# A hybrid encoder on one core: weight differences tied to a later tile of the weight stream

## The chip, the core and the metric

The kernel runs on one core of a Trainium2 chip. Its time is the device time of one execution in microseconds (us). The engines named below are TensorE (PE; its weight loads are listed apart as PEld), VectorE (DVE), ScalarE (ACT), GpSimd (POOL) and SyncE (SP). DMAs are issued from SP's and ACT's queues; a line "SPq" or "ACTq" in the profile is such an issue, and it stands in its engine's program order.

## The reference

Two encoder layers run over 272 tokens (16 meta tokens and 256 real ones) of width 2048, in float32. Cut to what matters here:

```python
h = rmsnorm(x); q, k, v, f, ga, gf = split(h @ W_in)
a = attention(q, k, v) @ W_attn_br          # grouped heads, rotary positions
s = real(fft2(f)) @ W_four                  # over positions and group channels
x = x + (sigmoid(ga) * a + sigmoid(gf) * s) @ W_out
up = rmsnorm(x) @ W_up                      # 2048 -> 2 x 5632
x = x + (silu(dwconv3(up[gate])) * up[val]) @ W_down
```

The weights of both layers are read once; the output is the 256 real tokens after the second layer.

## The kernel before

**Weights as a stream.** All weight matrices are cut into tiles of 128 x 1024 numbers (512 KB). One list, `order`, fixes the sequence of all tiles over the whole kernel. A tile `i` goes through three steps: `load_raw` fetches it by a DMA from SP into one of four `raw` buffers; `split_w` has ACT cast it to `wh` (line 230, its high part in the fast float32 format) and DVE subtract to get `wl` (line 233, the low part); then PE multiplies with both. `wh` and `wl` have three buffers each, so a cast waits until PE is done with the tile three places before it. `advance` and `pump` emit the split of a tile two tiles ahead of the one that PE works on.

**Products.** `group` runs one group of tiles: for each 128 x 128 block three matmuls, high x high, high x low and low x high (lines 304 to 306), 24 matmuls in a tile when the moving side is 272 tokens wide. After every second block it calls `step()` and `pump()`, so there are four steps to a tile. `st["cur"]` holds the `wh` of the tile that PE is on.

**Side work.** `step()` moves side work forward: generators yield the number of steps that they want to wait. `weight_sums` is one of these. It is put into the list `behindhand` when the feed-forward stage of the first layer begins, with 24 steps to wait, and so runs beside the `ug`, `uv` and `d` groups of that layer (gate half, value half, down projection).

**The weight differences.** In the second layer a part of the down projection is done as a product of 2 x 2 blocks with seven multiplications instead of eight (a Strassen form, `PRODUCTS`). It needs differences of weight blocks, which are made here ahead of time: for each of 16 rounds `q`, four blocks `b0` to `b3` of 128 x 1024 numbers are loaded from `w_blk`, four differences are made on DVE, and these are stored to device memory (`tsum`), where the second layer reads them as weight tiles. Loads and stores (lines 977 and 982) are issued from ACT's queue. Ahead of each load, a copy of one column from `st["cur"]` into the buffer (line 976) ties the load to a place in the weight stream. A difference (line 980) is emitted nine steps after the load of its second block.

**Who sets the order.** Within the limits of data and buffers, a planner lays down the order of the instructions on each engine when the program is built, by its own costs for each; an instruction may come earlier on its engine than it stands in the code, if by these costs its inputs are there. On the chip each engine then goes through its list in that order.

**Places.** Tiles are put at byte places in the order in which their pools are opened: `per` and `wp` first, then `small`, then a pool for each stage (`mix`, `ffn`). Tables such as `WL_AT`, `X_AT` and `G_AT` set the offsets of operands within their buffers by some tens of bytes.

Of the kernel before, what the change touches and what calls it, by code (L numbers as in the profile page):

```python
# [10 lines left out]
F32 = mybir.dt.float32  # L11
F32R = mybir.dt.float32r
AF = mybir.ActivationFunctionType
ALU = mybir.AluOpType
AX = mybir.AxisListType

P = 128
D = 2048
# [17 lines left out]
NPR = sum(FF_SPLIT[-1][:2]) // 2  # L36
# [84 lines left out]
def encoder_kernel(ctx, tc, xT, params, consts, bmat, w_in, w_abr, w_four, w_f64, w_out, w_up, w_down, w_blk, outT):  # L121
    nc = tc.nc
    dram = ctx.enter_context(tc.tile_pool(name="dram", bufs=1, space=bass.MemoryType.DRAM))
    tsum = [[dram.tile([P, D // 2], F32, name=f"ts{q}_{e}") for e in range(4)] for q in range(NPR)]
# [58 lines left out]
    st = {"raw": 0, "fetch": 0, "next": 0, "grp": 0}  # L183
# [13 lines left out]
    def advance(upto):  # L197
        while st["raw"] < min(upto + RAW, len(chunks)):
            load_raw(st["raw"])
            st["raw"] += 1  # L200
        while st["fetch"] < min(upto, len(chunks)):
            i = st["fetch"]
            if i in folded:
                todo.append((i, lambda i=i: fold_w(i)))
            todo.append((i, lambda i=i: split_w(i, 0, CW)))
            st["fetch"] += 1
# [14 lines left out]
    def split_w(i, a, b, eng=None):  # L221
        if i not in splits:
            h = wp.tile([P, CW, MG * P], F32R, tag="wh", name=f"wh{i}")
            lo = wp.tile([P, CW * MG * P + 64], F32R, tag="wl", name=f"wl{i}")
            o = wl_at[i]
            splits[i] = h, lo[:, o:o + CW * MG * P].rearrange("p (c m) -> p c m", c=CW)
        h, lo = splits[i]
        r = raws[i]
        if eng is None:
            nc.scalar.copy(h[:, a:b], r[:, a:b])  # L230
        else:
            eng.tensor_copy(h[:, a:b], r[:, a:b])
        nc.vector.tensor_tensor(lo[:, a:b], r[:, a:b], h[:, a:b].bitcast(F32), op=ALU.subtract)  # L233
        if b == CW:
            del raws[i]
# [112 lines left out]
    def first_groups(pss):  # L348
# [17 lines left out]
        for i, c0, c1, ks in ((0, 0, 1, (0,)), (0, 1, 2, (1,)), (1, 0, 2, ()), (0, 2, 4, (2, 3)), (1, 2, 4, ())):  # L366
            for k in ks:
                norm_split(k, P_NM)
            split_w(i, c0, c1, nc.vector if (i, c0) == (0, 0) else None)
# [56 lines left out]
    small = ctx.enter_context(tc.tile_pool(name="small", bufs=4))  # L426
# [92 lines left out]
    for l in range(DEPTH):  # L519
# [7 lines left out]
        with tc.tile_pool(name=f"mix{l}", bufs=1) as mp:  # L527
# [394 lines left out]
            for half in range(2):  # L922
                mH = mL = None
                for kind, i in BRANCH_ORDER[half]:
# [19 lines left out]
                    else:  # L944
# [6 lines left out]
                        for m in range(MG):  # L951
                            k = 2 * j + m
                            t_, h_ = tha[i][:, m, lo:T], mH[:, k, lo:T]
# [13 lines left out]
        with tc.tile_pool(name=f"ffn{l}", bufs=1) as fp:  # L967
# [2 lines left out]

            def weight_sums():
                tt = nc.vector.tensor_tensor
                for q in range(NPR):
                    b = [fp.tile([P, D // 2], F32, tag=f"b{e}", name=f"b{e}") for e in range(4)]
                    for e, sums in ((0, ()), (1, ((0, 1, 0, 0),)), (3, ((1, 3, 1, 1), (3, 3, 0, 2))), (2, ((2, 2, 3, 3),))):
                        nc.scalar.copy(b[e][:, 0:1], st["cur"][:, 0, 0:1].bitcast(F32))
                        nc.scalar.dma_start(b[e], w_blk[2 * q + e // 2, e % 2])
                        yield 9
                        for o, x, y, to in sums:
                            tt(b[o], b[x], b[y], op=ALU.subtract)  # L980
                            yield 2
                            nc.scalar.dma_start(tsum[q][to], b[o])
                        yield 3

            sets, prods = [], {"have": {}}
            if last:
# [79 lines left out]
            if l == DEPTH - 2:  # L1066
                behindhand.append([24, weight_sums()])
# [142 lines left out]
```

## Time and profile before

| | |
|---|---|
| runs | 2525.16, 2524.92 and 2531.62 us, median 2525.16 |
| the profiled execution | 2528.11 us, its span 2526.0 us |
| granted PE clock, mean | 0.999 |
| busy: PE, DVE, ACT | 99%, 73%, 51% of the span |
| DMA | 557.63 MB, mean 221 GB/s |
| loads of `b`, stores of `ts` | 64 and 64 of 512 KB, 5.0 and 3.6 us to landing (median) |

The span runs from the first to the last instruction. A row of a group lists line, engine, operation, output and inputs, shapes and count, then busy time and the mean of one in ns, then the idle time of the engine ahead of these instructions and who ended most of it. A row of a wait lists who waited for whom, the total, how often and the longest. A row of a timeline lists start, length, engine, line and operation, and in brackets the idle time before it and what ended it.

### The profile page before, as it was taken

What the parts mean: (1) busy time and instruction counts of PE and PEld (TensorE: products, weight loads), DVE (VectorE), ACT (ScalarE), POOL (GpSimd) and SP (SyncE); (2) the same over time, 40 slices, a digit from 0 to 9 for tenths busy, and PEclk for the clock granted to TensorE, in tenths of its full rate; (3) what the DMA queues carried; (4) which work ended last, traced back from release to release, by engine and by line L of the source; (5) the groups of instructions that cost most, each with busy time, mean ns of one, the idle gap of its engine ahead of it and who ended that gap; (6) DMA issues with size and microseconds to landing.
All of it is one profiled execution on the core that took longest, in us unless ns stands there. A gap on an engine that the chain in (4) does not pass through costs nothing.

```text
span 2526.0 us, 47879 instructions
## 1 busy us (share of the span) xinstructions
PE 2511.2 (99%) x19404; PEld 2441.2 (97%) x19404; DVE 1852.2 (73%) x2851; ACT 1276.4 (51%) x1857; POOL 18.3 (1%) x37
## 2 busy tenths in 40 slices
PE   9999999999999999999999999999999999999999
PEld 9999999999999999999999999999999989988888
DVE  7687867776776556676556887677766788879985
ACT  6455544554444334444444564445644565556653
POOL 0000000000000000000000000000000000000000
PEclk9999999999999999999999999999999999999999
DMA  7545666568888887787554555666656677778875
GB/s 240 166 157 161 194 185 190 189 225 283 286 282 281 277 292 266 270 288 266 183 179 151 175 157 188 196 201 200 188 189 192 217 243 247 244 249 256 260 244 174
DMA packets 157501, 557.63 MB, mean 221 GB/s; under 512 B 18144, under 2 KB 22112, under 8 KB 157280
## 3 DMA queue, kind: packets, MB, share of 16 engines
q1 hardware_dynamic: 134480, 482.54, 59.5%
q10 hardware_dynamic: 22800, 72.04, 8.1%
q8 instruction: 152, 2.49, 0.4%
q14 instruction: 69, 0.57, 0.1%
HBM read 516.07 MB, written 35.65 MB: 218 GB/s over the span
## 4 chain that ended last, share of the span: by engine, by line
PE 95%; DVE 2%; DMA 1%; ACT 1%; issue 1%; ACTq 0%; SPq 0%; DVEq 0%
PE ps_ug L306 6%; PE ps_ug L304 6%; PE ps_uv L300 6%; PE ps_ug L305 6%; PE ps_x L1046 6%; PE ps_d L306 4%; PE ps_d L304 4%; PE ps_d L305 4%; PE ps_uv L301 3%; PE ps_uv L306 3%; PE ps_uv L304 3%; PE ps_uv L305 3%; PE ps_o L304 2%; PE ps_o L306 2%; PE ps_o L305 2%; PE ps_gf L304 2%
## 5 line engine op out<-in xcount | busy, mean ns | idle before, releaser
L233 DVE TENSOR_TENSOR wl<-raw,wh 128x1024 fp32r<-128x1024 f32 (+1 forms) x883 | 1073.8, 1220 | 442.5 <-ACT wh L230 438.2
L230 ACT CAST wh<-raw 128x1024 fp32r<-128x1024 f32 (+1 forms) x882 | 920.9, 1046 | 853.6 <-PE ps_ug L305 171.4
L306 PE MATMUL ps_ug<-xHL,wl 128*128 128x272 f32 (+1 forms) x1408 | 397.6, 282 | 2.7 <-DVE wl L233 2.7
L304 PE MATMUL ps_ug<-xHL,wh 128*128 128x272 f32 (+1 forms) x1408 | 399.1, 283 | 0.0
L305 PE MATMUL ps_ug<-xHL,wh 128*128 128x272 f32 (+1 forms) x1408 | 397.1, 282 | 0.0
L306 PEld LDWEIGHTS ps_ug<-xHL,wl 128*128 128x128 f32 x1408 | 264.5, 188 | 3.1 <-DVE wl L233 3.1
L305 PEld LDWEIGHTS ps_ug<-xHL,wh 128*128 128x128 f32 x1408 | 264.8, 188 | 2.2
L304 PEld LDWEIGHTS ps_ug<-xHL,wh 128*128 128x128 f32 x1408 | 264.3, 188 | 2.7
L300 PE MATMUL ps_uv<-xHL,wh 128*128 128x512 f32 x704 | 247.7, 392 | 0.0
L306 PE MATMUL ps_d<-gHL,wl 128*128 128x272 f32 (+1 forms) x728 | 208.3, 286 | 2.5 <-DVE wl L233 2.5
L304 PE MATMUL ps_d<-gHL,wh 128*128 128x272 f32 (+1 forms) x728 | 208.8, 287 | 0.0
L305 PE MATMUL ps_d<-gHL,wh 128*128 128x272 f32 (+1 forms) x728 | 207.4, 285 | 0.0
L304 PE MATMUL ps_uv<-xHL,wh 128*128 128x272 f32 x704 | 201.3, 286 | 0.0
L306 PE MATMUL ps_uv<-xHL,wl 128*128 128x272 f32 x704 | 200.7, 285 | 0.0
L305 PE MATMUL ps_uv<-xHL,wh 128*128 128x272 f32 x704 | 199.9, 284 | 0.0
L301 PE MATMUL ps_uv<-xHL,wl 128*128 128x256 f32 x704 | 198.3, 282 | 0.0
L300 PEld LDWEIGHTS ps_uv<-xHL,wh 128*128 128x128 f32 x704 | 132.0, 188 | 28.6
L1046 PE MATMUL ps_x<-wh,cb 128*128 128x512 f32 x448 | 156.6, 393 | 0.0
L304 PE MATMUL ps_ga<-xHL,wh 128*128 128x272 f32 (+1 forms) x512 | 147.0, 287 | 0.0
L304 PE MATMUL ps_gf<-xHL,wh 128*128 128x272 f32 (+1 forms) x512 | 145.8, 285 | 0.1
L304 PE MATMUL ps_o<-mH,wh 128*128 128x272 f32 (+1 forms) x512 | 144.6, 282 | 0.0
L306 PE MATMUL ps_ga<-xHL,wl 128*128 128x272 f32 (+1 forms) x512 | 144.6, 282 | 0.0
(306 smaller groups left out, 5979.8 us busy)
## 6 DMA issues: line engine op xcount, KB each, us to landing
raw<-in_w_up SPq DMA_DIRECT2D x352, 512.0 KB, 4.4
raw<-in_w_in SPq DMA_DIRECT2D x206, 512.0 KB, 3.6
raw<-in_w_down SPq DMA_DIRECT2D x112, 512.0 KB, 4.3
raw<-in_w_out SPq DMA_DIRECT2D x64, 512.0 KB, 3.9
b<-in_w_blk ACTq DMA_DIRECT2D x64, 512.0 KB, 5.0
ts<-b ACTq DMA_DIRECT2D x64, 512.0 KB, 3.6
raw<-ts SPq DMA_DIRECT2D x64, 512.0 KB, 4.5
raw<-in_w_blk SPq DMA_DIRECT2D x48, 512.0 KB, 4.4
```

The costliest lines, as they stand in the source:

```text
L230: nc.scalar.copy(h[:, a:b], r[:, a:b])
L233: nc.vector.tensor_tensor(lo[:, a:b], r[:, a:b], h[:, a:b].bitcast(F32), op=ALU.subtract)
L300: nc.tensor.matmul(o2, h[:, c, sl], ab, start=kt == 0, stop=False)
L301: nc.tensor.matmul(o, lo[:, c, sl], ab[:, 0, :], start=False, stop=kt == nk - 1)
L304: nc.tensor.matmul(o, h[:, c, sl], a, start=kt == 0, stop=False)
L305: nc.tensor.matmul(o, h[:, c, sl], b, start=False, stop=False)
L306: nc.tensor.matmul(o, lo[:, c, sl], a, start=False, stop=kt == nk - 1)
L1046: nc.tensor.matmul(ps[e], cb[:, s_, q - q4], w, start=q == 0 and a == 0, stop=q == n - 1 and a == 2)
```

## The change

The first feed-forward stage still makes the same differences from the same blocks. In `split_w`, `st["new"]` now remembers the `wh` of the newest tile whose split has been emitted. In `weight_sums`, the differences of a block are no longer emitted behind its own load. They are kept in a list `due`, and come five steps after the load of the next block. Ahead of them ACT writes a column `one`: the value 1.0, computed as 0 x (first column of `st["new"]`) + 1.0, so that it cannot be written before that tile's cast. The difference is then a `scalar_tensor_tensor` on DVE, `x * one - y`, which reads this column. Two differences that fall due together share one column. The steps between the parts are set so that each of the four blocks of a round takes 12 steps (they were 12, 14, 16 and 14), and one last part round makes the last difference. `one` has two buffers of 128 bytes in the pool `small`, 256 bytes in all, so that the pools behind it move by 256 bytes.

```diff
@@ split_w
             o = wl_at[i]
+            st["new"] = h
             splits[i] = h, lo[:, o:o + CW * MG * P].rearrange("p (c m) -> p c m", c=CW)
@@ weight_sums
-                for q in range(NPR):
-                    b = [fp.tile([P, D // 2], F32, tag=f"b{e}", name=f"b{e}") for e in range(4)]
+                b, due = {}, []
+                for q in range(NPR + 1):
                     for e, sums in ((0, ()), (1, ((0, 1, 0, 0),)), (3, ((1, 3, 1, 1), (3, 3, 0, 2))), (2, ((2, 2, 3, 3),))):
-                        nc.scalar.copy(b[e][:, 0:1], st["cur"][:, 0, 0:1].bitcast(F32))
-                        nc.scalar.dma_start(b[e], w_blk[2 * q + e // 2, e % 2])
-                        yield 9
-                        for o, x, y, to in sums:
-                            tt(b[o], b[x], b[y], op=ALU.subtract)
-                            yield 2
-                            nc.scalar.dma_start(tsum[q][to], b[o])
-                        yield 3
+                        if q < NPR:
+                            t_ = fp.tile([P, D // 2], F32, tag=f"b{e}", name=f"b{e}")
+                            nc.scalar.copy(t_[:, 0:1], st["cur"][:, 0, 0:1].bitcast(F32))
+                            nc.scalar.dma_start(t_, w_blk[2 * q + e // 2, e % 2])
+                        yield 5
+                        if due:
+                            one = small.tile([P, 32], F32, tag="one", name="one", bufs=2)[:, 0:1]
+                            nc.scalar.activation(one, st["new"][:, 0, 0:1].bitcast(F32), AF.Identity, bias=1.0, scale=0.0)
+                        for o, x, y, to in due:
+                            nc.vector.scalar_tensor_tensor(o, x, one, y, op0=ALU.mult, op1=ALU.subtract)
+                            yield 3
+                            nc.scalar.dma_start(to, o)
+                        if q == NPR:
+                            return
+                        b[e] = t_
+                        yield 7 - 3 * min(len(due), 2)
+                        due = [(b[o], b[x], b[y], tsum[q][to]) for o, x, y, to in sums]
```

## The prediction

> **What bounds the kernel now.** I read the page first (busy times and the chain that ended last), then the waits of TensorE (PE) alone, then busy time by stretches of the span, then the order of instructions around one wait. From the page:
>
> ```profile
> span 2526.0 us, 47879 instructions
> ...
> PE 2511.2 (99%) x19404; PEld 2441.2 (97%) x19404; DVE 1852.2 (73%) x2851; ACT 1276.4 (51%) x1857; POOL 18.3 (1%) x37
> ...
> PE 95%; DVE 2%; DMA 1%; ACT 1%; issue 1%; ACTq 0%; SPq 0%; DVEq 0%
> ```
>
> PE is the bound; VectorE (DVE) and ScalarE (ACT) have room. The edit adds no matmul and takes none away, so it can move the time only through moments in which PE stands still or runs slower. Its place is the first layer's feed-forward stage. All waits of PE from 525 to 1300 us are these:
>
> ```profile
> PE ps_ug L306 <- DVE wl L233: 2.7, 2, 1.7
> PE ps_d L306 <- DVE wl L233: 2.5, 1, 2.5
> ```
>
> Three waits, 5.2 us, each for the low part `wl` of a weight tile. Busy time by stretch (columns: length, then busy time and instruction count of each engine, granted PE clock, DMA share, GB/s):
>
> ```profile
> 530.00:700.00 170.00, 170.00 (x1392) 169.92 (x1391) 122.22 (x166) 81.73 (x120) 0.85 (x1) 1.00 0.80 278
> 700.00:1010.00 310.00, 310.00 (x2537) 309.83 (x2536) 201.79 (x240) 134.36 (x181) 0.00 (x0) 1.00 0.82 279
> 1010.00:1197.00 187.00, 181.86 (x1470) 181.22 (x1469) 129.31 (x170) 84.03 (x122) 0.00 (x0) 0.99 0.80 274
> 1197.00:1300.00 103.00, 103.00 (x845) 103.00 (x844) 59.78 (x78) 47.30 (x64) 0.00 (x0) 1.00 0.57 186
> 1187.00:1191.00 4.00, 4.00 (x21) 4.00 (x21) 3.36 (x6) 1.72 (x5) 0.00 (x0) 0.57 0.93 310
> ```
>
> Undisturbed, one matmul takes 310/2537 = 0.1222 us, and 103/845 = 0.1219 us with the differences gone: their traffic by itself does not slow PE. Between 1010 and 1197 us, 1470 matmuls should have taken 1470 x 0.1222 = 179.6 us and took 187: **7.4 us lost**. 5.2 us are the three waits; another 1.4 us lie behind the last of them, where the granted clock is 0.57 and 21 matmuls run in 4 us instead of 32.7; 0.8 us go in starting again.
>
> What is late in the last wait is seen in its order on ACT, DVE and PE:
>
> ```profile
> 1176.38 0.34 ACTq L977 DMA_DIRECT2D b<-in_w_blk  x1
> 1177.91 1.22 DVE L233 TENSOR_TENSOR wl<-raw,wh 128x1024 fp32r<-128x1024 f32 x1
> 1184.35 1.23 DVE L980 TENSOR_TENSOR b<-b,b 128x1024 f32<-128x1024 f32 x1 [4.86 <-DMA b<-in_w_blk]
> 1185.49 1.22 DVE L233 TENSOR_TENSOR wl<-raw,wh 128x1024 fp32r<-128x1024 f32 x1
> 1186.04 1.04 ACT L230 CAST wh<-raw 128x1024 fp32r<-128x1024 f32 x1 [6.63 <-DVE b L980]
> 1186.77 0.39 PE L306 MATMUL ps_d<-gHL,wl 128*128 128x272 f32 x1 [2.46 <-DVE wl L233]
> ```
>
> The difference L980 stands on DVE one `wl` split behind the issue of its load, waits 4.86 us for that load, and holds the next split; its store, issued from ACT, holds the next cast for 6.63 us. Over the stage:
>
> ```profile
> DVE b L980 <- DMA b<-in_w_blk: 69.3, 44, 4.9
> ACT wh L230 <- DVE b L980: 30.2, 8, 6.6
> DMA to landing us min/median/max: 3.4/5.0/7.9
> 1169.50 1.23 DVE L980 TENSOR_TENSOR b<-b,b 128x1024 f32<-128x1024 f32 x1 [3.74 <-DMA b<-in_w_blk]
> ```
>
> (The third row is that of the loads at L977.) 44 of 64 differences wait, but only three reach PE: a hold of 3.74 us still costs nothing, one of 4.86 us costs 2.46 us.
>
> **The change, part by part.** *Distance.* Steps of the generator come every six matmuls, 6 x 0.1222 = 0.733 us, four to a tile, so a tile lasts 2.93 us. Loads are anchored on the tile under multiplication (`cur`); they come at steps 24 + 12k, the last step of a tile t. The sum comes 17 steps later, in the first step of tile t+5, and its column is written from the newest split, t+6. The planner that lays down the order of each engine can therefore put load and difference no closer than six tiles, 6 x 2.93 = 17.6 us; so far it put them about two apart, though 9 steps lie between them in the program. Against a longest landing of 7.9 us the load is in with 9.7 us to spare, even if it is issued two tiles late (3.8 us then). I take the whole of the 69.3 us of waits as gone, with the three that reach PE and the slow clock behind the last: **-7.4 us**. Bounds: 0 (something else holds DVE as long) and -7.4 us.
>
> *Next late.* Then the split itself waits only for its cast, which PE paces. The column is an ACT instruction just behind the cast that DVE also needs for the `wl` of that tile; the column's 0.19 us passes while DVE does that split, so the wait for it should be near zero.
>
> *New and changed instructions.* From the groups of the stage:
>
> ```profile
> L233 DVE TENSOR_TENSOR wl<-raw,wh 128x1024 fp32r<-128x1024 f32 x262 | 320.6, 1224 | 170.1 <-ACT wh L230 169.1
> L230 ACT CAST wh<-raw 128x1024 fp32r<-128x1024 f32 x262 | 274.2, 1047 | 297.1 <-PE ps_d L305 123.2 <-PE ps_ug L305 77.7 <-PE ps_uv L305 41.0
> L980 DVE TENSOR_TENSOR b<-b,b 128x1024 f32<-128x1024 f32 x64 | 78.4, 1224 | 69.7 <-DMA b<-in_w_blk 69.3
> L1130 DVE TENSOR_TENSOR gHL<-cv,gHL 128x272 fp32r<-128x272 f32 x44 | 19.2, 436 | 2.2 <-ACT gHL L1129 1.5
> L480 DVE SCALAR_TENSOR_TENSOR xHL<-XT,prm,xHL 128x272 fp32r<-128x272 f32 x15 | 7.4, 495 | 0.0
> L976 ACT COPY b<-wh 128x1 f32<-128x1 f32 x64 | 12.1, 189 | 1.5
> L1111 ACT ACT_TABLE_LOAD x1 | 1.3, 1283 | 0.0
> ```
>
> 48 columns (three of four blocks in each of 16 rounds) at about 0.19 us, the copy at L976, are 9 us of ACT; Identity runs beside Silu in this stage already, with one table load in all, so I add none. 64 differences become scalar_tensor_tensor. At 272 elements that form takes 495 against 436 ns; if the 59 ns are fixed it is 1.28 us, if they grow with length 1.224 x 495/436 = 1.39 us, and 1.22 us if they vanish. I take 1.28: +4 us of DVE (0 to +11). Both are covered: DVE is busy 122.22 + 201.79 + 129.31 = 453 of 667 us, ACT 300. Without that cover the most they would add is 9 + 11 = 20 us.
>
> *Pace.* A round had 12 + 14 + 16 + 14 = 56 steps and has 4 x 12 = 48, so the stage of differences ends at step 24 + 768 + 8 = 800 instead of 920. Loads and stores are as many as before:
>
> ```profile
> L977 ACTq DMA_DIRECT2D b<-in_w_blk x64: 334/339/344, 533.1 to 1191.2; - x64
> q10 hardware_dynamic: 18288, 66.59, 27.9%
> 1191.00:1195.00 4.00, 4.00 (x35) 4.00 (x34) 2.56 (x3) 2.03 (x4) 0.00 (x0) 1.00 0.97 352
> DMA to landing us min/median/max: 3.3/4.6/7.8
> ```
>
> From the first load, 776 steps or 569 us are left: 66.6 MB plus 194 weight tiles of 0.524 MB (101.7) make 296 GB/s, where 279 ran without a PE wait and 352 were reached for 4 us. The last row is the landing of the weight tiles: they have four buffers, so 4 x 2.93 - 1.05 - 1.22 = 9.4 us from issue to use, against 7.8 us at the worst. I take 0. The last load moves from 1191 to about 533 + 756 x 0.733 = 1087 us.
>
> *Places.* The 256 bytes move every tile of the later pools by the same amount; no row shows what a shift does, so I take 0.
>
> *Sum.* The profiled execution took 2528.11 us (span 2526.0 and 2.1 around it): 2528.11 - 7.4 = 2520.7, with 0.3 for small new waits 2521.0. The three runs shown have a median of 2525.16, 2.95 us under the profiled one, so an ordinary run seems to carry some 4.5 us of these waits. Against the median the forecast is -4.2 us, 0.17%; I call 0.3% (7.6 us) the least that a measurement of this kernel tells from no change.
>
> [...] The row has the granted clock fall to 0.57 behind a PE wait of 2.46 us. [...] The trace speaks for the wait as its cause, since no other stretch of this stage shows a lower clock.
>
> **The rivals.** *Another hold takes the place (about 2527 us).* The next round's copy into `b0` must wait for the second of two differences (`b3 - b0`), which shares its column with the first. Behind the same cast DVE does one split and two differences, 1.22 + 2 x 1.28 = 3.8 us, just what PE bore (3.74). If the planner puts that copy ahead of the next cast, ACT holds it so long in each of 16 rounds; 0.4 us each, half a split, make 6.4 us: 2520.7 + 6.4 = 2527. For it: ACT stood behind DVE 30.2 us in eight places. Against it: there a DMA was in the hold, here none.
>
> *The weight tiles come late (about 2555 us, the slower side).* If the DMA engines cannot hold more than the 279 GB/s of the quiet stretch, 168.3 MB take 603 us instead of 569: +34 us. It decides where a weight tile takes more than 9.4 us to land. Against it: 352 GB/s in one stretch, and a mean share that would rise only to 0.82 x 296/279 = 0.87. [...]
>
> *It does not do what it says.* A column at the wrong tile would leave the distance near two and the time at 2525; the step count above excludes it unless a load slips by four tiles.
>
> *More goes than these waits (about 2517 us).* The second layer still has
>
> ```profile
> PE ps_s L340 <- DVE wl L233: 1.8, 3, 0.8
> PE ps_pt L853 <- DVE pn L844: 0.8, 1, 0.8
> ```
>
> and a newly laid order might drop these: 2520.7 - 2.6 = 2518.1, a little lower with luck. Nothing in the edit aims there.
>
> **How the numbers follow.** Forecast (waits gone, 2518 to 2524): 0.62. Another hold or no effect (2524 to 2532): 0.17. More gained, below 2517.6: 0.12. Slower than 2532.7, by late weights or shifted places: 0.09. So faster 0.12, same 0.79, slower 0.09. The range 2516 to 2529 takes in the forecast, the second layer's waits and the new hold, and leaves out the upper tail.
>
> **What would show it.** Right: no PE wait for `wl` between 525 and 1300 us, granted clock 1.00 throughout, the differences waiting for neither load nor column, last load near 1087 us, DMA near 296 GB/s until then. Wrong: PE waits there again (behind a copy or store on ACT: the new hold; behind a weight tile's DMA: the slower rival), or matmul steps other than 0.1222 us (the places).

## The result, and the profile after

The changed kernel takes 2520.09 us (median of 8 runs, 2518.88 to 2521.61) against 2525.55 us before (8 runs, 2523.85 to 2532.36). The ratio is 0.9973, 95% interval 0.9962 to 0.9985: a real gain of about 5.5 us, inside the 0.3% that the prediction calls no change. The profiled execution took 2520.25 us, 7.86 us less than the one before. The kernel before also spreads over 8.5 us from run to run and the changed one over 2.7.

The page of the changed kernel (its lines have moved down by one, in the feed-forward part by ten; L234 is the old L233, L231 the old L230; in `weight_sums` L980 is now the load of a block, L984 the column and L986 the difference):

```profile
span 2518.3 us, 47970 instructions
...
PE 2507.6 (100%) x19404; PEld 2438.7 (97%) x19404; DVE 1855.8 (74%) x2851; ACT 1282.2 (51%) x1905; POOL 18.3 (1%) x37
...
PE 97%; DVE 2%; ACT 1%; DMA 0%; issue 0%; SPq 0%; DVEq 0%; ACTq 0%
```

All waits of PE over the whole span:

```profile
PE ps_f L362 <- ACT wh L231: 4.1, 4, 1.5
PE ps_s L341 <- DVE wl L234: 1.6, 3, 0.8
PE ps_idle L433 <- DVE ones L429: 1.1, 1, 1.1
PE ps_ss L688 <- DVE sqm L781: 0.3, 1, 0.3
```

The three waits of `ps_ug` and `ps_d` for `wl` are gone; between 525 and 1300 us PE waits for nothing. The same stretches as before, cut where the differences now end (length, busy time and count of each engine, granted clock, DMA share, GB/s):

```profile
700.00:1010.00 310.00, 310.00 (x2539) 310.00 (x2538) 211.67 (x249) 139.09 (x215) 0.00 (x0) 1.00 0.86 299
1010.00:1110.00 100.00, 100.00 (x821) 100.00 (x820) 74.77 (x96) 47.68 (x76) 0.00 (x0) 1.00 0.86 294
1110.00:1197.00 87.00, 87.00 (x715) 87.00 (x714) 52.74 (x74) 39.47 (x52) 0.00 (x0) 1.00 0.55 185
```

Between 1010 and 1197 us, 821 + 715 = 1536 matmuls run instead of 1470, at the same 0.122 us each, and the granted clock is 1.00. By stage, measured from the first matmul of one to the first of the next, the second half of the first layer's up groups fell from 238.16 to 234.67 us and the down projection behind it from 121.65 to 117.33: together 7.8 us, nearly all of the 7.86 us between the two profiled executions. Elsewhere the stages differ by 1.0 us at most, with both signs (the start of the kernel +1.0, the second layer's q groups -1.0).

One difference in the order of ACT and DVE:

```profile
543.33 0.33 ACTq L980 DMA_DIRECT2D b<-in_w_blk  x1
544.89 1.05 ACT L231 CAST wh<-raw 128x1024 fp32r<-128x1024 f32 x1 [1.59 <-PE ps_uv L306]
...
559.84 1.03 ACT L231 CAST wh<-raw 128x1024 fp32r<-128x1024 f32 x1
561.62 0.19 ACT L984 ACTIVATE one<-wh 128x1 f32<-128x1 f32 x1
562.89 1.28 DVE L986 SCALAR_TENSOR_TENSOR b<-b,one,b 128x1024 f32<-128x1024 f32 x1
564.20 0.34 ACTq L988 DMA_DIRECT2D ts<-b  x1
```

Six casts lie between the load of its second block and the column (the first and last are shown), and the difference starts 19.6 us behind that load, waiting for nothing. Over the stage (waits and rows of single lines):

```profile
DVE b L986 <- ACT one L984: 2.9, 5, 0.6
L986 DVE SCALAR_TENSOR_TENSOR b<-b,one,b x64: 1276/1280/1285, 562.9 to 1107.7; 128x1024 f32<-128x1024 f32 x64
L984 ACT ACTIVATE one<-wh x48: 185/203/204, 561.6 to 1106.5; 128x1 f32<-128x1 f32 x48
L980 ACTq DMA_DIRECT2D b<-in_w_blk x64: 334/335/344, 534.0 to 1089.2; - x64
DMA to landing us min/median/max: 4.0/5.8/8.4
```

The waits for loads (69.3 us) have become 2.9 us for the column. The loads themselves land later than before (median 5.8 us against 5.0), but no difference waits for them.

### The profile page after: what moved, and what is told of

It is laid out like the page before. It is cut to its first block, busy times and chain, and to the rows that moved or that the text cites. A ratio compares the mean times of both kernels' runs of the same rounds, so it can differ in the third digit from the quotient of the medians.

```text
span 2518.3 us, 47970 instructions
## 1 busy us (share of the span) xinstructions
PE 2507.6 (100%) x19404; PEld 2438.7 (97%) x19404; DVE 1855.8 (74%) x2851; ACT 1282.2 (51%) x1905; POOL 18.3 (1%) x37
## 4 chain that ended last, share of the span: by engine, by line
PE 97%; DVE 2%; ACT 1%; DMA 0%; issue 0%; SPq 0%; DVEq 0%; ACTq 0%
PE ps_ug L305 7%; PE ps_ug L307 7%; PE ps_ug L306 7%; PE ps_uv L301 6%; PE ps_x L1056 6%; PE ps_d L307 4%; PE ps_d L305 4%; PE ps_d L306 4%; PE ps_uv L307 3%; PE ps_uv L305 3%; PE ps_uv L306 3%; PE ps_uv L302 3%; PE ps_o L305 2%; PE ps_o L307 2%; PE ps_o L306 2%; PE ps_gf L305 2%
## 5 line engine op out<-in xcount | busy, mean ns | idle before, releaser
L234 DVE TENSOR_TENSOR wl<-raw,wh 128x1024 fp32r<-128x1024 f32 (+1 forms) x883 | 1073.7, 1220 | 480.6 <-ACT wh L231 476.5
L231 ACT CAST wh<-raw 128x1024 fp32r<-128x1024 f32 (+1 forms) x882 | 921.3, 1047 | 849.4 <-PE ps_ug L306 190.6
```

## The experiments

The theory: what pays is the distance in weight tiles between a load and its difference; the column is only the means by which the planner is made to keep it. Rivals: the later place in the program is enough (A); the even, faster pace pays (B). "Tiles between" below is counted in the order of each engine's instructions: `wl` splits ahead of the difference on DVE that belong to casts behind the load of its second block on ACT. By this count the kernel before has one tile between in 53 of the 64 differences and two in 11; the changed kernel has six in 47, five in 5 and seven in 12, and the shortest time from load to difference is 16.7 us.

### The late place without the column

```diff
-                            one = small.tile([P, 32], F32, tag="one", name="one", bufs=2)[:, 0:1]
-                            nc.scalar.activation(one, st["new"][:, 0, 0:1].bitcast(F32), AF.Identity, bias=1.0, scale=0.0)
+                            small.tile([P, 32], F32, tag="one", name="one", bufs=2)
...
-                            nc.vector.scalar_tensor_tensor(o, x, one, y, op0=ALU.mult, op1=ALU.subtract)
+                            tt(o, x, y, op=ALU.subtract)
```

> The changed kernel without its column: the differences stand as late in the program (17 steps behind their load, 12 steps a block) but are a plain subtraction that waits for nothing in the weight stream. Theory (the distance in tiles between load and difference, which only the column imposes, is what pays): the planner draws each difference forward to about one tile behind its load, DVE waits for the loads again (50 to 100 us in all, longest 4 to 6 us), PE waits for wl in the first feed-forward stage 2 to 6 times, time 2524 to 2535 us. Rival A (the later place in the program is enough): no such waits, 2519 to 2522 us. Rival B (the even pace of 12 steps is what pays): also 2519 to 2522 us.

2527.42 us, ratio to before 1.0004 (0.9996 to 1.0013). All 64 differences stand one tile behind their load, although the program has them 17 steps later. Waits of PE and DVE in the stage (L985 is the difference):

```profile
PE ps_uv L307 <- DVE wl L234: 2.1, 4, 0.9
PE ps_ug L307 <- DVE wl L234: 1.9, 4, 0.7
DVE b L985 <- DMA b<-in_w_blk: 58.1, 46, 3.6
```

Rival A falls: the planner undoes the later place. The number of PE waits was expected as 2 to 6 and is 8, each shorter than those before; the longest wait for a load was expected as 4 to 6 us and is 3.6. The listed waits are not the whole loss: measured by first matmuls as above, the first layer's up groups and down projections take 8.7 us longer than in the changed kernel, and the eight waits sum to 4.0. A wait costs more than its length (in the kernel before, the one of 0.96 us at 1017.75 us costs 1.2 us with the slower steps around it), and stalls below 0.15 us stand in no list of waits.

### The column written at the load, and five steps behind it

```diff
+                            if sums:
+                                one = ones_[e] = small.tile([P, 16], F32, tag="one", name="one", bufs=4)[:, 0:1]
+                                nc.scalar.activation(one, st["new"][:, 0, 0:1].bitcast(F32), AF.Identity, bias=1.0, scale=0.0)
...
-                        due = [(b[o], b[x], b[y], tsum[q][to]) for o, x, y, to in sums]
+                        due = [(b[o], b[x], b[y], tsum[q][to], ones_[e]) for o, x, y, to in sums]
```

In the second of the two, the first three lines stand behind the `yield 5`. In both, the column ahead of the differences is left out, a difference reads the column of its own block, and four buffers of 64 bytes again make 256 bytes.

> The changed kernel, but each column is written at the step of its block's own load, from the newest split then, two tiles on; the differences keep form, count and place in the program. Theory: the difference may now stand two tiles (5.9 us) behind its load; the median landing of 5.0 us fits, the longest of 7.9 us does not, so DVE waits for loads in a few places (5 to 25 us in all, longest under 3.7 us), which PE bears: 2519 to 2523 us, between the two kernels but near the changed one. Rival A or B (late place or even pace): no difference from the changed kernel at all, no waits for loads.

> As the run before, with each column written five steps behind its block's load, from three tiles on (8.8 us). Theory: more than the longest landing, so no difference waits for its load (under 3 us in all), no PE wait for wl in the stage, 2518.5 to 2522 us as with six tiles. Against the theory would be: waits as with one tile.

With the column at the load: 2519.74 us, 0.9977 (0.9968 to 0.9986), one to three tiles between (36 of 64 have two). Five steps behind: 2519.78 us, 0.9975 (0.9965 to 0.9984), three to four tiles between. The stage of the first, and the only PE waits for a `wl` split that the second has left, in the second layer:

```profile
PE ps_ug L307 <- DVE wl L234: 1.4, 1, 1.4
DVE b L986 <- DMA b<-in_w_blk: 27.7, 14, 4.5
```

```profile
PE ps_s L341 <- DVE wl L234: 1.7, 3, 0.8
```

At one tile the differences wait 58 to 69 us for loads, at two 27.7 us (14 places, the longest 4.5 us; 5 to 25 us and a longest under 3.7 were expected), at three and six not at all. Two tiles cost one PE wait of 1.4 us in the profiled execution, where none was expected, and nothing that the times show; three are enough.

### The pace alone, in both directions

The kernel before with 12 steps a block, and the changed kernel with 14:

```diff
-                        yield 9
+                        yield 9 - len(sums) // 2
...
-                            yield 2
+                            yield 2 - len(sums) // 2
...
-                        yield 3
+                        yield (3, 1, 2)[len(sums)]
```

```diff
-                        yield 7 - 3 * min(len(due), 2)
+                        yield 9 - 3 * min(len(due), 2)
```

> The kernel before, its steps between the parts set so that each block takes 12 steps, as in the changed kernel; nothing else changed. Theory: distance stays one tile, so DVE waits for loads in at least as many places as before (60 to 110 us in all), PE waits for wl 3 to 8 times, 2525 to 2540 us. Rival B (the pace pays): 2519 to 2522 us.

> The changed kernel at the pace before, 14 steps a block or 56 a round; column and order of parts as changed. Theory (distance pays, pace does not): no PE wait for wl in the stage, 2518.5 to 2522 us. Rival B (the faster, even pace pays): part of the gain is lost, 2522 to 2526 us.

Before at the new pace: 2527.19 us, 1.0001 (0.9991 to 1.0010). Changed at the old pace: 2519.33 us, 0.9976 (0.9963 to 0.9988). Rival B falls on both sides. In the first, the same four stages take 9.2 us longer than in the changed kernel, with listed PE waits of 4.3 us. The stage of the first, then all PE waits for `wl` of the second:

```profile
PE ps_uv L306 <- DVE wl L233: 2.7, 5, 1.0
PE ps_ug L306 <- DVE wl L233: 0.9, 2, 0.8
PE ps_d L306 <- DVE wl L233: 0.7, 1, 0.7
DVE b L980 <- DMA b<-in_w_blk: 59.8, 44, 3.9
```

```profile
PE ps_s L341 <- DVE wl L234: 1.7, 3, 0.8
```

### A denser stream of differences

```diff
-                        yield 5
+                        yield 3
...
-                            yield 3
+                            yield 2
...
-                        yield 7 - 3 * min(len(due), 2)
+                        yield 5 - 2 * min(len(due), 2)
```

> The changed kernel at 8 steps a block instead of 12 (32 a round): loads and stores of the differences half again as dense, some 350 GB/s in the stage; the column now lies about three to five tiles behind the load. It tests the slower rival of the prediction. Theory (DMA engines are full near 350 GB/s): weight tiles or loads come late in places, PE waits, 2522 to 2545 us. If the DMA engines bear it, no PE wait and 2519 to 2522 us.

2539.27 us, 1.0053 (1.0037 to 1.0070). A stretch of the stage, and what ACT waits for:

```profile
700.00:930.00 230.00, 218.20 (x1742) 214.03 (x1741) 155.78 (x179) 95.88 (x168) 0.00 (x0) 1.00 0.93 334
ACT b L979 <- DMA ts<-b: 78.8, 22, 5.8
ACT b L979 <- DVE b L986: 16.5, 12, 4.6
ACT wh L231 <- DMA raw<-in_w_up: 7.9, 7, 1.6
```

The DMA engines are 93% busy at 334 GB/s (the 350 GB/s of the theory were estimated from the kernel before, where they were 97% busy at 352 GB/s from 1191 to 1195 us), and PE loses 11.8 of 230 us. But what ACT waits for most is not the weight tiles (7.9 us): the copy ahead of a load stands on ACT until the store from the same `b` buffer has landed (78.8 us), and holds the casts behind it. Which share is owed to the fuller DMA engines and which to the five to nine steps less between a store and the next load into its buffer (11 instead of 16 for `b0` and `b1`), this run does not tell apart.

### What hold of DVE PE bears

A hold is a time for which DVE is kept from its next `wl` split. The reductions that are added lengthen it in steps:

```diff
+                        if e == 0 and q in (3, 5, 7, 9, 11, 13, 15):
+                            n_ = 1024 * (q + 1) // 2
+                            nc.vector.tensor_reduce(one_[:, 1:2], one.to_broadcast([P, n_]), axis=AX.X, op=ALU.max)
```

> The changed kernel with seven added reductions on DVE, one in every second round from the fourth on, that read the column 2048, 3072, ... 8192 times and so hold DVE for about 2.1 to 8.6 us each, directly ahead of a difference of about 1.3 us; results are not touched. It measures what hold of DVE PE bears, and what a PE wait does to the granted clock. Theory: a hold of 3.4 us (the first) costs nothing, each further one about its length less 3.8 us (0.7, 1.8, 2.8, 3.9, 5.0, 6.0), some 20 us in all, and PE waits longer than about 2.4 us are followed by a stretch of 3.4 us at half the clock that costs 1.4 to 1.6 us more each: 2540 to 2550 us. If the slow stretch in the profile before had another cause than the wait, no lower clock shows here: 2538 to 2542 us. [...]

2532.53 us (one run), less than the 2540 to 2550 us expected. The fourth and sixth reductions on DVE, and the PE waits behind the fourth to the seventh:

```profile
860.31 5.48 DVE L988 TENSOR_REDUCE one<-one 128x1 f32<-128x5120 f32 x1
1004.15 7.61 DVE L988 TENSOR_REDUCE one<-one 128x1 f32<-128x7168 f32 x1
868.17 0.52 PE L307 MATMUL ps_d<-gHL,wl 128*128 128x272 f32 x2 [0.71 <-DVE wl L234]
940.62 0.52 PE L307 MATMUL ps_d<-gHL,wl 128*128 128x272 f32 x2 [1.77 <-DVE wl L234]
1014.14 0.53 PE L307 MATMUL ps_uv<-xHL,wl 128*128 128x272 f32 x2 [2.84 <-DVE wl L234]
1090.34 0.79 PE L307 MATMUL ps_uv<-xHL,wl 128*128 128x272 f32 x2 [3.91 <-DVE wl L234]
```

The first three, up to 4.41 us and a difference, cost nothing; from 5.48 us on each further 1.07 us of hold is 1.07 us of wait. With the difference behind it (1.2 us), a hold of some 6 us is borne here, not 3.8. The granted clock behind the waits of 1.77, 2.84 and 3.91 us (the last figure but two of each row):

```profile
940.62:950.00 9.38, 9.38 (x76) 9.38 (x77) 5.40 (x6) 2.97 (x3) 0.00 (x0) 1.00 0.91 323
1015.30:1018.70 3.40, 3.40 (x17) 3.40 (x17) 3.40 (x7) 1.89 (x5) 0.00 (x0) 0.50 0.79 224
1090.40:1093.80 3.40, 3.40 (x15) 3.40 (x16) 3.40 (x8) 1.62 (x5) 0.00 (x0) 0.50 0.86 271
```

The two longer waits are followed by 3.4 us at half the clock, the one of 1.77 us is not.

### The places

The column tile of 2 x 32 and of 2 x 64 bytes instead of 2 x 128:

```diff
-                            one = small.tile([P, 32], F32, tag="one", name="one", bufs=2)[:, 0:1]
+                            one = small.tile([P, 8], F32, tag="one", name="one", bufs=2)[:, 0:1]   # and [P, 16]
```

> The changed kernel with a column tile of 32 bytes in each of its two buffers instead of 128, so that the pools behind it move by 64 bytes instead of 256, if the tiles are not padded. The prediction took the shift of places at nothing: then 2518.5 to 2522 us and 0.122 us a matmul in every stretch. If places count, the matmul step changes in stretches that read the later pools, the down projections above all, and the time by several us either way.

> The changed kernel with a column tile of 2 x 64 bytes, so that the later pools move by 128 bytes. If places count by a period of 128 bytes or less, it is as with 256 bytes: 2518.5 to 2522 us and 0.1222 us a matmul in the first layer's down projection. If the period is 256 bytes, that step is longer there, 0.123 us or more, and the time 2522 to 2532 us.

2529.13 us, 1.0014 (1.0005 to 1.0023), and 2531.62 us, 1.0022 (1.0013 to 1.0031): all of the gain and more is lost, with no PE wait for `wl` in the stage. The first layer's down projection, 810 to 940 us, before and with a shift of 256, 64 and 128 bytes:

```profile
810.00:940.00 130.00, 130.00 (x1066) 130.00 (x1065) 74.69 (x73) 48.71 (x58) 0.00 (x0) 1.00 0.85 286
810.00:940.00 130.00, 130.00 (x1066) 130.00 (x1065) 77.95 (x74) 50.13 (x70) 0.00 (x0) 1.00 0.87 304
810.00:940.00 130.00, 130.00 (x1047) 130.00 (x1047) 77.28 (x74) 50.08 (x69) 0.00 (x0) 1.00 0.86 296
810.00:940.00 130.00, 130.00 (x1038) 130.00 (x1037) 77.92 (x75) 49.09 (x71) 0.00 (x0) 1.00 0.86 292
```

PE is busy throughout in all four, but a matmul takes 0.1220 us unshifted and at 256 bytes, 0.1242 at 64 and 0.1252 at 128. The stretch from the first layer's o groups to its first up group grows too, from 203.9 to 206.1 us with either shift; the up groups of the first layer, whose operands lie in earlier pools, do not change: from 530 to 800 us, 2209 matmuls run at a shift of 256 bytes, 2209 at 64 and 2210 at 128.

One stage of the 64-byte run was shorter: the second layer's up groups with their block products. So that stage's last buffers alone were moved, among them `cb`, the only one of them that PE reads:

```diff
                 if last and c:
+                    if c == 1:
+                        fp.tile([P, 16], F32, name="shift1")
                     push(combos(c - 1), 2)
```

> The changed kernel with a tile of 64 bytes put ahead of the buffers that the second layer's feed-forward stage takes from its second part on (the split operands cb of the block products, and the output buffers), so that these alone move by 64 bytes. With the column tile of 2 x 32 bytes the first and second layer's down projections and the o groups were slower, but the second layer's up stage was 2.43 us shorter (646.92 against 649.35 us). If that came from the place of cb, the up stage is 2.4 us shorter here too and nothing else changes: 2516.5 to 2519 us. If it came from operands allocated earlier (the gate set, C4, u, cv), nothing changes: 2519 to 2521 us.

2517.29 us, 0.9965 (0.9953 to 0.9977), the fastest of all. The second layer's up stage in the changed kernel and in this one:

```profile
1796.00:2445.30 649.30, 649.30 (x4199) 590.89 (x4198) 513.28 (x674) 376.22 (x473) 0.85 (x1) 1.00 0.73 233
1795.40:2442.30 646.90, 646.90 (x4200) 587.97 (x4199) 513.46 (x674) 375.97 (x473) 0.85 (x1) 1.00 0.74 234
```

The same 4200 matmuls in 2.4 us less. That it is `cb` and not another of the moved buffers is argued from who reads it, not shown.

## Why the prediction was right, point by point

- **Distance.** Shown, though "no closer than six tiles" is a little too strict: 47 of 64 differences have six tiles between, five have five, and the closest stands 16.7 us behind its load where 17.6 was the least. No difference waits for its load. The runs at one, two, three and six tiles give the waits for loads as 58 to 69, 27.7, 0 and 0 us; the time falls from one tile to two and stays there. Six is more than needed.
- **The sum.** -7.4 us against the profiled execution; that one fell by 7.86 us, 7.8 of it in the two stages named. The forecast of 2521.0 us was met by 2520.09. The medians differ by 5.5 us where 4.2 were worked out. An ordinary run may carry more of these waits than the 4.5 us inferred from the gap between the median and the profiled run; no ordinary run was traced, so this is not shown.
- **The clock behind the last wait.** The 1.4 us were rightly counted with the wait: the stage now shows 1.00 throughout. The holds confirm it, with 3.4 us at half clock behind PE waits of 2.84 and 3.91 us and none behind 1.77. In these traces 2.46 us (before) and 2.84 us (the holds) were enough; in the 3.4 us ahead of the slow stretch these waits left PE idle for 2.46 and 2.24 us (last section).
- **Cost of the new instructions.** The difference was put at 1.28 us and takes 1.280; the column at 0.19 and takes 0.203; both stay covered.
- **Pace.** Last load expected near 1087 us, seen at 1089.2; 296 GB/s expected, 299 and 294 seen. No weight tile came late (no wait of ACT for a `raw` load from 525 to 1300 us), and the pace by itself moves nothing (2527.19 us with the new pace alone, 2519.33 with the old pace and the column).
- **The bearing of a hold** was mis-sized: "a hold of 3.74 us still costs nothing, one of 4.86 us costs 2.46 us" was read as if 3.8 us were the limit. Without the column, DVE waits of at most 3.6 us let PE wait eight times; with the holds in a quiet place, some 6 us were borne. That it depends on how far ahead the splits stand when the hold begins is argued, not shown. The limit did not enter the sum, only the first rival.
- **The rivals.** The new hold did come on ACT, and PE bore it. These are the waits of the copies in the stage:

```profile
ACT b L979 <- DVE cv L1122: 3.8, 5, 0.8
ACT b L979 <- DVE gHL L1140: 2.2, 6, 0.4
```

All 11 are copies into `b0`. The two operations named work on neither `b0` nor the weights; in each case they stand on DVE directly behind `b3 - b0`, the last reader of that buffer, so the copy is taken to wait for this difference. The sum of 6.0 us is near the 6.4 us of this rival, but no PE wait follows: what failed in it is the step from a late cast to PE. When the stream is made denser, late weight tiles are the smaller part (7.9 us on ACT against 95.3 us for the `b` buffers).

- **Places at nothing.** Right for 256 bytes by luck, since no row of the trace gave a reason; the shifts by 64 and 128 bytes cost 9.0 and 11.5 us, more than the whole gain.

## What to carry to other kernels

Where a planner orders instructions by its own idea of how fast a DMA lands, an instruction that is merely written later in the program is drawn forward again; tie it to data of a later place in the stream that the bounding engine paces, and give it more than the longest landing rather than the median: two tiles, 5.9 us against a longest landing of 7.9, left one PE wait in the stage here, three left none. A wait on an engine that is not the bound costs only what reaches the bound (in the kernel before DVE waited 69.3 us for loads and PE 5.2 us behind it), so read the waits of the bounding engine first and follow one of them back. Any added tile moves those behind it: keep the shift at a multiple that the operands' places bear (256 bytes did here), and check the time of one matmul per stage after each edit.

## What the runs showed of the hardware that was not expected

In the first layer's down projection the time of a matmul went with the bytes by which the later pools were moved: 0.1220 us unshifted and at 256 bytes, 0.1242 at 64 and 0.1252 at 128, with PE busy and the clock at 1.00 in all. A period of 64 or 128 bytes does not fit these four numbers; one of 256 does, but no other multiple of it was run. Why the place matters is not settled here.

Behind the first 10 us of a run, half the clock followed PE waits of 2.46, 2.84 and 3.91 us and none of those up to 1.77 us. The first row below is the slow stretch of the kernel before, 3.41 us long. The others are of that length too: the stretch ahead of it, the one ahead of the first slow stretch in the run with holds, and two over which the wait of 1.77 us is spread (length, then PE's busy time):

```profile
1187.59:1191.00 3.41, 3.41 (x17) 3.41 (x16) 2.77 (x6) 1.64 (x4) 0.00 (x0) 0.50 0.92 296
1184.17:1187.59 3.42, 0.96 (x8) 0.83 (x7) 3.24 (x3) 1.04 (x1) 0.00 (x0) 1.00 0.36 145
1011.90:1015.31 3.41, 1.17 (x9) 1.17 (x10) 3.41 (x5) 0.83 (x2) 0.00 (x0) 1.00 0.46 163
936.81:940.22 3.41, 2.04 (x17) 1.82 (x15) 3.41 (x3) 1.24 (x2) 0.00 (x0) 1.00 0.00 0
940.22:943.63 3.41, 3.01 (x24) 3.01 (x25) 2.62 (x3) 0.37 (x1) 0.00 (x0) 1.00 1.01 321
```

PE was idle for 72% and 66% of the two stretches ahead of half a clock, and for 40% and 12% of the last two, behind which the clock stayed at 1.00 (row from 940.62 to 950 us above). Whether the length of a wait or PE's idle share of such a stretch decides, and where between these numbers the border lies, the runs do not tell.
